# Decoder layer on one Trainium2 core: three folded FFN tiles instead of four

## The chip, the cores and the metric

One core of a Trainium2 chip runs the whole layer in one launch. The metric is device time in microseconds of that core. The runs shown are three of the kernel before, median 1054.19 (1053.89 to 1054.98). One execution was recorded by the hardware profiler; it took 1052.81.

The engines are called as in the profile: PE is TensorE (PEld its weight loads), DVE is VectorE, ACT is ScalarE, POOL is GpSimd, SP is SyncE, which only issues the weight transfers here.

## The reference, cut to what matters

A decoder layer for 272 tokens (16 meta tokens and 256) of width 2048: sparse attention and a pooling mixer, then an output projection with a residual and a layer norm, then a gated FFN with a causal convolution of width 3, and a second residual and layer norm. The part around the change:

```python
h = layer_norm(ALPHA * h + mix, ln1_g, ln1_b)
z = h @ w_up                                       # 2048 -> 2 * 5632
z = sum(zp[:, j:j + T] * conv_w[j] for j in range(3)) + conv_b
a, g = jnp.split(z, 2, axis=-1)
f = (jax.nn.gelu(a) * g) @ w_down
h = layer_norm(ALPHA * h + f, ln2_g, ln2_b)
```

## The kernel before, in words

Activations stand transposed, features on the 128 partitions and tokens along the row; 258 of the tokens are kept for the FFN. A matmul in full precision is made of three: weights and activations are split in a high and a low part, and high by high, high by low and low by high are summed in PSUM (lines 187 to 189 in `product`). A weight tile is 128 x 2048. SP loads it, and `fetch` splits it in two halves of 1024 columns: ACT copies the high part (line 123), DVE subtracts for the low part (line 124). The tiles come in one fixed stream, and `weights()` asks for each two places ahead of its use, from three buffers.

The FFN has 44 tiles of 128 hidden features. A tile `f` has two up-products of 48 matmuls, one for the value (`half_` 0) and one for the gate (`half_` 1). Then come the convolution (`conv`, lines 698 to 700: one ACT and two DVE instructions), the gelu and the product (`gate`, lines 715 and 716). Tiles are grouped in parts of eight. From the second part on the up-products alternate with down-products of the part before (lines 763 to 765). These take seven products where eight stand in the definition, from sums and differences of gated tiles. `forms` makes the sums for two tiles at a time: four instructions on POOL (735 to 738), then `two_parts`, the split of what they give, on ACT (721) and DVE (722). Their buffers are in two groups: `gp`, sixteen of them, and `acc`, one.

The layer norm before the FFN needs sums over all features, and they are known only when the output projection is done. So that PE need not wait, the first tiles are *folded*: their products take the unnormalised residual sum, multiplied by the norm's gain, of which sixteen split copies `folded` stand in the sixteen `gp` buffers (260 columns: two more for gain and bias). `unfold` then puts the token's scale and mean into the product: on DVE a copy of two columns (706) and a multiplication (708), on ACT an affine row (710, in the `acc` buffer), on POOL an addition (711). Meanwhile `normalise` makes the sixteen normalised parts `h_parts`, three after each product (lines 680 on POOL, 681 on DVE, 682 and 684 on ACT, 685 on DVE), and the tiles from `FOLDED` on read those.

After the tiles `FOLDED` and `FOLDED + 1` DVE transposes the residual in blocks, eight instructions each (line 860), and in the six tiles from `FOLDED + 2` on, 32 DMAs issued from ACT's queue (line 692) move the blocks to `y2`, where the down-products are summed. The first sums of part 0 are added to `y2` at the end of tile 9, and its other half is first read at the end of tile 11.

The program is written in this order, and each engine takes its instructions in a fixed order that a scheduler made of it; an instruction that waits holds up what stands behind it on its engine. These lines set where the change acts:

```python
if todo and f > FOLDED - 1 + half_:
    p, r = todo.pop(0)
    pairs[p].append(forms(r, len(pairs[p]), p == FAST))
if f < FOLDED:
    ...
    product(ps[:, :NE], hl, P, folded, 0, NE, k0=k)
    while len(h_parts) < min(KT, 3 * (2 * f + half_ + 1)):
        normalise(len(h_parts))
    ...
else:
    product(ps[:, :NQ], hl, P, h_parts, 0, NQ)
```

Of the kernel before, what the change touches and what calls it, by code (L numbers as in the profile page):

```python
# [33 lines left out]
FT = FF // P  # L34
PARTS = (8, 8, 8, 8, 8, 4)
FAST = 4
FOLDED = 4
MF = 80 + C
NE = NQ + 2
ALPHA = 2.0 ** 0.25  # L40
# [27 lines left out]
def tile_layer(ctx, tc, xt, w_first, w_proj, w_uk, w_uv, w_pool, w_o, w_up, w_down, cols, rows, rel_bias, onehot, out):  # L68
# [8 lines left out]
    def big():  # L77
        return pm.tile([P, 512], F32, tag="mm", name="mm")
# [652 lines left out]
    def forms(r, j, whole):  # L731

        a11, a21, a12, a22 = r[:, 0, :P], r[:, 0, P:], r[:, 1, :P], r[:, 1, P:]
        s = fp.tile([P, 4 * P], F32, name="forms", tag="acc", bufs=1).rearrange("p (a b) -> p a b", b=P)
        nc.gpsimd.tensor_tensor(s[:, 0], a21, a22, op=ALU.add)  # L735
        nc.gpsimd.tensor_tensor(s[:, 2], s[:, 0], a11, op=ALU.subtract)
        nc.gpsimd.tensor_tensor(s[:, 1], a12, s[:, 2], op=ALU.subtract)
        nc.gpsimd.tensor_tensor(s[:, 3], a11, a21, op=ALU.subtract)  # L738
        left = two_parts(slot(), r[:, :, :P])
        mid = two_parts(slot(), s[:, :2])  # L740
        right = ring.tile([P, 2, T], F32R, tag="act", name="right")
        right = two_parts(right[:, :, :2 * P].rearrange("p a (b c) -> p a b c", c=P), s[:, 2:])
        if j % 2 == 0:
            held["lone"], held["other"] = slot(), slot() if whole else None
        two_parts(held["lone"][:, :, j % 2], a22)
        if whole:
            two_parts(held["other"][:, :, j % 2], a21)
        return {"P1": (left, 0), "P2": (left, 1), "P5": (mid, 0), "P3": (mid, 1), "P6": (right, 0),
                "P7": (right, 1), "P4": (held["lone"], j % 2),
                "a11": (left, 0), "a12": (left, 1), "a21": (held["other"], j % 2), "a22": (held["lone"], j % 2)}  # L750
# [44 lines left out]
    for item in plan:  # L795
# [32 lines left out]
        ps = big()  # L828
# [4 lines that stand above are left out]
            k = 0  # L833
# [22 lines left out]
        elif f % 2:  # L856
            todo.append((part, pair))
        if f in (FOLDED, FOLDED + 1):
            for m in range(8 * (f - FOLDED), 8 * (f - FOLDED) + 8):
                nc.vector.transpose(y[:, m, NM:], y[:, m, NM:])  # L860
        if FOLDED + 2 <= f < FOLDED + 8:
            for _ in range((6, 5, 5)[f % 3]):
# [153 lines left out]
```

## Time and profile before

| what | value |
|---|---|
| median of three runs | 1054.19 us |
| the profiled execution, its time | 1052.81 us |
| the profiled execution, its span | 1051.0 us |
| granted TensorE clock over the span | 0.996 |
| first folded matmul | 306.7 us |
| first matmul that reads `h_parts` | 357.5 us |
| last matmul of the up-products | 993.6 us |
| moved by DMA, mean rate | 249.75 MB, 238 GB/s |

The span is the time from the first instruction to the last; the rest of the profiled execution's time lies around it. Rows of a timeline give start and duration in microseconds, engine, line, operation, the tile written and the tiles read, and in brackets the idle time of the engine before the instruction and what ended it. Matmuls are pipelined, and a duration of 0.28 is not the pace: that is read from start to start. Instructions of DVE overlap by some 0.08 in the same way. Groups of instructions give the busy time, the mean duration of one in ns and, behind the second bar, the idle time before them.

### The profile page before, as it was taken

The numbers are of one execution on the slowest core, as the hardware profiler recorded it, in microseconds if no ns is written. First come the engines' busy times: TensorE is split into PE (matmuls) and PEld (weight loads), VectorE is DVE, ScalarE is ACT, GpSimd is POOL, SyncE is SP. The second block draws the span as 40 slices with busy tenths as digits, with TensorE's granted clock in tenths as the row PEclk, the third lists the DMA queues.
The fourth block names the chain that finished last, engine by engine and source line by source line (L and its number), as shares of the span: only waits on it lengthen the run. The fifth ranks groups of instructions, "written<-read, shape, count | busy, mean of one in ns | idle before, by whom it ended". The sixth has DMA issues, their size and how long they took to land. (4 is left out here: it accounts for less than half of the span.)

```text
span 1051.0 us, 19241 instructions
## 1 busy us (share of the span) xinstructions
PE 1037.5 (99%) x7671; PEld 986.4 (94%) x7671; DVE 888.7 (85%) x1381; ACT 620.7 (59%) x998; POOL 214.0 (20%) x264
## 2 busy tenths in 40 slices
PE   9999999999999999999999999999999999999996
PEld 8998999999999999999999999999999999999985
DVE  6879468858779987898999989898998998989876
ACT  7666345745447765565665655556655665556673
POOL 1100014125436231201112021120211221220030
PEclk9999999999999999999999999999999999999998
DMA  9756542454552577898897787877878778788764
GB/s 322 255 172 237 190 152 96 148 189 164 193 193 89 201 217 213 276 310 261 275 300 270 284 275 264 289 274 270 284 268 290 270 281 275 271 280 272 285 210 141
DMA packets 59322, 249.75 MB, mean 238 GB/s; under 512 B 21686, under 2 KB 22112, under 8 KB 32224
## 3 DMA queue, kind: packets, MB, share of 16 engines
q1 hardware_dynamic: 34160, 229.76, 60.5%
q0 software_dynamic: 7600, 15.62, 7.8%
q10 hardware_dynamic: 17472, 3.15, 1.6%
q8 instruction: 60, 0.98, 0.4%
q14 instruction: 30, 0.25, 0.1%
HBM read 232.50 MB, written 2.11 MB: 223 GB/s over the span
## 5 line engine op out<-in xcount | busy, mean ns | idle before, releaser
L124 DVE TENSOR_TENSOR whl<-wraw,whl 128x1024 fp32r<-128x1024 f32 (+1 forms) x416 | 489.2, 1212 | 49.0 <-ACT whl L123 46.8
L123 ACT ACTIVATE whl<-wraw 128x1024 fp32r<-128x1024 f32 (+1 forms) x416 | 402.6, 1015 | 120.3 <-DVE wraw L119 26.4
L188 PE MATMUL mm<-hp,whl 128*128 128x258 f32 x1280 | 362.4, 283 | 0.0
L189 PE MATMUL mm<-hp,whl 128*128 128x258 f32 x1280 | 361.3, 282 | 0.8 <-DVE whl L124 0.8
L187 PE MATMUL mm<-hp,whl 128*128 128x258 f32 x1280 | 361.5, 282 | 0.2 <-ACT whl L123 0.2
L187 PEld LDWEIGHTS mm<-hp,whl 128*128 128x128 f32 x1280 | 242.5, 189 | 3.6 <-ACT whl L123 0.4
L188 PEld LDWEIGHTS mm<-hp,whl 128*128 128x128 f32 x1280 | 242.7, 190 | 3.1
L189 PEld LDWEIGHTS mm<-hp,whl 128*128 128x128 f32 x1280 | 242.9, 190 | 1.0 <-DVE whl L124 1.0
L187 PE MATMUL mm<-xp,whl 128*128 128x256 f32 (+5 forms) x384 | 111.2, 290 | 0.0
L188 PE MATMUL mm<-xp,whl 128*128 128x256 f32 (+5 forms) x384 | 108.9, 284 | 0.0
L189 PE MATMUL mm<-xp,whl 128*128 128x256 f32 (+5 forms) x384 | 108.7, 283 | 0.0
L698 ACT ACTIVATE z<-mm,cv 128x256 f32<-128x256 f32 x40 | 22.6, 564 | 91.4 <-PE mm L189 90.5
L188 PEld LDWEIGHTS mm<-xp,whl 128*128 128x128 f32 x384 | 72.3, 188 | 0.8 <-issue 0.5
L187 PEld LDWEIGHTS mm<-xp,whl 128*128 128x128 f32 x384 | 72.4, 188 | 0.6
L189 PEld LDWEIGHTS mm<-xp,whl 128*128 128x128 f32 x384 | 72.4, 189 | 0.3 <-DVE whl L124 0.2
L738 POOL TENSOR_TENSOR forms<-za 128x128 f32<-128x128 f32 x20 | 26.4, 1321 | 221.8 <-DVE za L716 214.3
L764 PE MATMUL at<-whl,gp 128*128 128x512 f32 x180 | 71.2, 396 | 0.0
L765 PE MATMUL at<-whl,gp 128*128 128x512 f32 x180 | 71.1, 395 | 0.0
L763 PE MATMUL at<-whl,gp 128*128 128x512 f32 x180 | 71.0, 395 | 0.0
L698 ACT ACTIVATE za<-mm,cv 128x256 f32<-128x256 f32 x40 | 22.5, 562 | 58.4 <-PE mm L189 58.4
L735 POOL TENSOR_TENSOR forms<-za 128x128 f32<-128x128 f32 x20 | 21.8, 1089 | 104.4 <-DVE za L716 104.3
L765 PEld LDWEIGHTS at<-whl,gp 128*128 128x128 f32 x180 | 33.8, 188 | 8.0
(327 smaller groups left out, 1942.7 us busy)
## 6 DMA issues: line engine op xcount, KB each, us to landing
wraw<-in_w_up SPq DMA_DIRECT2D x88, 1024.0 KB, 5.1
wraw<-in_w_down SPq DMA_DIRECT2D x80, 1024.0 KB, 6.5
wraw<-in_w_proj SPq DMA_DIRECT2D x24, 1024.0 KB, 5.0
wraw<-in_w_o SPq DMA_DIRECT2D x16, 1024.0 KB, 4.8
y<-v POOLq DMA_DIRECT2D x27, 256.0 KB, 8.4
y<-u POOLq DMA_DIRECT2D x18, 256.0 KB, 4.8
wraw<-in_w_first SPq DMA_DIRECT2D x8, 304.0 KB, 5.3
x<-in_xt SPq DMA_DIRECT2D x1, 2176.0 KB, 8.7
```

What stands on the lines that cost most here:

```text
L123: nc.scalar.activation(hl[:, 0, c], raw[:, c], AF.Copy)
L124: nc.vector.tensor_tensor(hl[:, 1, c], raw[:, c], hl[:, 0, c].bitcast(F32), op=ALU.subtract)
L187: nc.tensor.matmul(ps, wh, ah, start=n == 0, stop=False)
L188: nc.tensor.matmul(ps, wh, al, start=False, stop=False)
L189: nc.tensor.matmul(ps, wl, ah, start=False, stop=n == KT - 1)
L698: nc.scalar.activation(z, src[:, 2:NQ], AF.Identity, bias=col(C_B, j), scale=col(C_W, 3 * j + 2))
L735: nc.gpsimd.tensor_tensor(s[:, 0], a21, a22, op=ALU.add)
L738: nc.gpsimd.tensor_tensor(s[:, 3], a11, a21, op=ALU.subtract)
L763: nc.tensor.matmul(ps, a[:, 0, i], hl[:, 0, w], start=j == 0, stop=False)
L764: nc.tensor.matmul(ps, a[:, 0, i], hl[:, 1, w], start=False, stop=False)
L765: nc.tensor.matmul(ps, a[:, 1, i], hl[:, 0, w], start=False, stop=j == n - 1)
```

## The change

One constant:

```diff
-FOLDED = 4
+FOLDED = 3
```

By it, the products of tile 3 (the fourth) read `h_parts`, 258 columns, and not `folded`, 260; its two `unfold` calls go, and `conv` reads the PSUM directly, as in the later tiles. The `forms` of tiles 0 and 1 are called before the first product of tile 3 and not of tile 4, those of tiles 2 and 3 before the first of tile 4 and not of tile 5; from the pair of tiles 4 and 5 on the calls stand as before. The sixteen transpositions of the residual come after tiles 3 and 4 (before: 4 and 5), and the 32 moves in the tiles 5 to 10 (before: 6 to 11). The `normalise` calls stay where they were: three after each of the first five products and the sixteenth after the second product of tile 2. The order of the weight stream and of PE's products is the same.

## The prediction

> **Names.** Tiles are counted from 0, as `f` is in the code: the change takes tile 3 out of the folded ones. A tile has two products, 3a and 3b for tile 3. A product is 48 matmuls: for each of 16 operands three, the third of which reads the low part of the weights.
>
> **What bounds the kernel now.** I read the page's totals first, then the table by stretches.
>
> ```profile
> PE 1037.5 (99%) x7671; PEld 986.4 (94%) x7671; DVE 888.7 (85%) x1381; ACT 620.7 (59%) x998; POOL 214.0 (20%) x264
> ```
>
> ```profile
> 300.00:350.00 50.00, 49.37 (x407) 48.44 (x405) 43.68 (x84) 33.40 (x61) 23.77 (x25) 1.00 0.40 132
> 350.00:400.00 50.00, 48.88 (x403) 48.25 (x402) 45.03 (x79) 32.40 (x53) 14.46 (x17) 1.00 0.70 221
> 400.00:450.00 50.00, 50.00 (x365) 47.46 (x364) 42.71 (x59) 29.36 (x43) 9.29 (x10) 1.00 0.83 253
> ```
>
> The columns of the stretches are microseconds, then busy time of PE, PEld, DVE, ACT, POOL, then clock, DMA share and GB/s. TensorE works 99% of the span at a granted clock of 1.00, and from 400 us on it has no gap. The changed code lies between 300 and 400, the only stretch hereabouts where it misses time (0.63 and 1.12 us). Whatever start tile 6 gets is therefore carried to the end. So I forecast one number, the start of 6a. The timeline of PE shows where each product begins:
>
> ```profile
> 345.68 0.28 PE L187 MATMUL mm<-fold,whl 128*128 128x260 f32 x1
> ...
> 351.08 0.28 PE L187 MATMUL mm<-fold,whl 128*128 128x260 f32 x1
> ...
> 351.43 0.29 PE L187 MATMUL mm<-fold,whl 128*128 128x260 f32 x1
> ...
> 351.90 0.39 PE L189 MATMUL mm<-fold,whl 128*128 128x260 f32 x1
> ...
> 357.54 0.28 PE L187 MATMUL mm<-hp,whl 128*128 128x258 f32 x1
> ...
> 369.01 0.29 PE L187 MATMUL mm<-hp,whl 128*128 128x258 f32 x1
> ...
> 375.23 0.39 PE L187 MATMUL mm<-hp,whl 128*128 128x258 f32 x1 [0.24 <-ACT whl L123]
> ...
> 376.55 0.39 PE L189 MATMUL mm<-hp,whl 128*128 128x258 f32 x1 [0.82 <-DVE whl L124]
> ...
> 382.15 0.28 PE L187 MATMUL mm<-hp,whl 128*128 128x258 f32 x1
> ```
>
> These are the starts of 3a (345.68) with its sixteenth operand (351.08), of 3b, 4a, 5a, 5b and 6a. 4a and 4b together take 369.01 - 357.54 = 11.47, so a product that waits for nothing takes 5.74. Against that, 3b took 6.11 (its third matmul waited for weights) and 5b began 0.48 late and took 6.92. The waits to be won are thus 0.37 + 0.48 + 1.18 = 2.03 us, all for weights that ACT (L123) and VectorE (L124) split too late. VectorE is the engine behind them:
>
> ```profile
> 348.10 0.42 DVE L685 TENSOR_TENSOR hp<-x,hp 128x258 fp32r<-128x258 f32 x1
> ...
> 350.66 2.32 DVE L124 TENSOR_TENSOR whl<-wraw,whl 128x1024 fp32r<-128x1024 f32 x2
> 352.89 0.97 DVE L685 TENSOR_TENSOR hp<-x,hp 128x258 fp32r<-128x258 f32 x1
> ...
> 364.53 1.41 DVE L860 STREAM_TRANSPOSE x<-x 128x256 f32<-128x256 f32 x4
> ...
> 371.83 0.42 DVE L722 TENSOR_TENSOR gp<-forms,gp 128x256 fp32r<-128x256 f32 x1 [1.76 <-ACT gp L721]
> ...
> 373.71 0.43 DVE L860 STREAM_TRANSPOSE x<-x 128x256 f32<-128x256 f32 x1
> ...
> 374.38 0.47 DVE L699 SCALAR_TENSOR_TENSOR za<-mm,cv,za 128x256 f32<-128x256 f32 x1
> ...
> 375.28 2.35 DVE L124 TENSOR_TENSOR whl<-wraw,whl 128x1024 fp32r<-128x1024 f32 x2
> 377.55 0.42 DVE L722 TENSOR_TENSOR gp<-forms,gp 128x256 fp32r<-128x256 f32 x1
> ```
>
> Its only long idle time is 1.76 us before 371.83, where it stands behind the forms of tiles 0 and 1; the weights of 5b are split after that, at 375.28, and 5b is the product that waits.
>
> **What goes.** Tile 3's two unfoldings take these away, twice each:
>
> ```profile
> L711 POOL TENSOR_TENSOR u<-u,w 128x258 f32<-128x258 f32 x8 | 10.4, 1306 | 29.1 <-ACT w L710 18.4 <-DVE u L708 9.4 <-issue 1.3
> L710 ACT ACTIVATE w<-of_token,sc 128x258 f32<-128x258 f32 x8 | 4.8, 598 | 0.8 <-DVE sc L706 0.7
> L708 DVE TENSOR_TENSOR u<-mm,of_token 128x258 f32<-128x258 f32 x8 | 3.3, 412 | 0.0
> ```
>
> That is 2 x 1.31 us of POOL, 2 x 0.60 of ACT and 2 x 0.41 of VectorE (the two-column copy of L706 beside it is smaller). The 96 matmuls of tile 3 are 258 columns wide instead of 260; 3a from 345.68 to 351.43 took 5.75 with 260, a free product 5.74 with 258, so this is worth at most 0.02. None of the removed work stands on PE's path by itself; it counts through the order of the weight splits, below.
>
> **What is added: 3a now reads the normalised parts.** Up to the sixteenth part the order of the instructions on ACT, VectorE and POOL is the same in both kernels, and nothing in front of it waits for 3a. So its times can be read off:
>
> ```profile
> 351.81 0.41 ACT L684 ACTIVATE hp<-x 128x258 fp32r<-128x258 f32 x1
> ...
> 353.62 0.60 ACT L698 ACTIVATE za<-u,cv 128x256 f32<-128x256 f32 x1 [0.45 <-POOL u L711]
> ```
>
> High part at 351.81 + 0.41 = 352.22, low part at 352.89 + 0.97 = 353.86. 3a wants the operand at 351.08 and its low part one matmul, 0.12, later. The fifteenth part and those ahead of it come before the pair of L124 at 350.66, in time. So 3a stands until 353.9, and 3b begins at about 354.15 instead of 351.43: **+2.72**.
>
> Then the wait of 3b goes, for its weights are split by 350.66 + 2.32 = 352.98: 4a begins at 354.15 + 5.74 = 359.89, **+2.35**. If nothing else waited, 5b would begin at 359.89 + 3 x 5.74 = 377.11 and 6a at 382.85, **+0.70**.
>
> **What is moved.** The forms of tiles 0 and 1 now stand at 3a, those of tiles 2 and 3 at 4a; the sixteen transposes stand behind tiles 3 and 4. What is queued behind each is a weight split, so I follow VectorE to the split of 5b. First the rows of POOL, then two of ACT:
>
> ```profile
> 352.03 1.55 POOL L711 TENSOR_TENSOR u<-u,w 128x258 f32<-128x258 f32 x1 [6.39 <-ACT w L710]
> 354.85 1.16 POOL L711 TENSOR_TENSOR u<-u,w 128x258 f32<-128x258 f32 x1 [1.27 <-ACT w L710]
> ...
> 368.46 1.33 POOL L735 TENSOR_TENSOR forms<-za 128x128 f32<-128x128 f32 x1
> ...
> 370.88 0.46 POOL L737 TENSOR_TENSOR forms<-za,forms 128x128 f32<-128x128 f32 x1
> ```
>
> ```profile
> 354.13 0.59 ACT L710 ACTIVATE w<-of_token,sc 128x258 f32<-128x258 f32 x1
> 354.62 1.05 ACT L123 ACTIVATE whl<-wraw 128x1024 fp32r<-128x1024 f32 x1
> ```
>
> 1. ACT ends L698 at 354.22, as before, but in the new order one half of 4a's weights (1.05) stands between it and L710 (0.59): L710 ends near 355.7. POOL's add of tile 2b, 1.16 to 1.55, ends at 356.9 to 357.3. The four forms behind it take 370.88 + 0.46 - 368.46 = 2.88, and VectorE begins on them 371.83 - 371.34 = 0.49 after: at 360.3 to 360.7. It waits some 2 us there, as it did before 371.83.
> 2. From there to the end of tile 3's gate (L716) stand, in the new order: five small instructions that are the same five as from 371.83 to 373.71 (1.88); L699 and L700 with one transpose (0.90 from 374.38 to 375.28, and 0.35 from 1.41 / 4); the split of 4b (375.28 to 377.55, 2.27); seven transposes (2.45); L699, L700 and a transpose again (1.25); half the split of 5a (1.14); L716 (0.42). Sum 10.66; with 0.4 less where an instruction of the old rows stood behind POOL, 10.3. L716 ends at 370.6 to 371.4. On the way the first half of 4b's split is done by 360.7 + 1.88 + 1.25 + 1.22 = 365.05 at the latest, and 4b wants it with its third matmul, 365.63 + 0.24; that of 5a is done by 371.0, wanted at 371.6. Both are just in time.
> 3. Behind that gate stand the second forms. The same order of instructions is to be seen two tiles later:
>
> ```profile
> 387.17 0.42 DVE L716 TENSOR_TENSOR za<-za,z 128x256 f32<-128x256 f32 x1
> ...
> 392.58 2.36 DVE L124 TENSOR_TENSOR whl<-wraw,whl 128x1024 fp32r<-128x1024 f32 x2
> ```
>
> From L716's end at 387.59 to the end of the first half split, 392.58 + 1.22 = 393.80, it is 6.21, with a wait of VectorE for POOL and ACT inside. Here two transposes (0.70) stand in it as well: 6.9. So 5b's first half is there at 377.5 to 378.3. 5b wants it with its third matmul, 377.11 + 0.24 = 377.35: a wait of 0.15 to 0.95, with some 0.1 more to get going again. I take 0.8, towards the later end, as two forms and two transposes are more than the row behind the pattern had. 6a begins at 382.85 + 0.8: **+1.5 us**.
>
> The row of 352.89 shows a second thing: the L685 took 0.97 there and 0.42 at 348.10, and POOL's add ran from 352.03 to 353.58. [...]
>
> **Later.** Residual moves are issued one tile earlier from ACT's queue, as many as before. In the old trace the last of them hold VectorE up (the first row below) without reaching PE:
>
> ```profile
> 475.95 0.69 DVE L771 SCALAR_TENSOR_TENSOR y<-y,v 128x512 f32<-128x512 f32 x1 [1.91 <-issue]
> ...
> 477.75 2.36 DVE L124 TENSOR_TENSOR whl<-wraw,whl 128x1024 fp32r<-128x1024 f32 x2
> ...
> 479.39 0.28 PE L187 MATMUL mm<-hp,whl 128*128 128x258 f32 x1
> ```
>
> The split's first half was there at 478.9, wanted at 479.63: 0.7 us of cover, and I price the move at nothing. Were that cover gone, each microsecond that VectorE loses more would be lost to PE. The moves land a tile earlier, so the wait of 1.91 should go and the cover grow.
>
> **The sum.** The profiled execution took 1052.81, its span 1051.0 and 1.8 around it: 1054.3 with 1.5 more. The median of the runs is 1.38 above that execution, so I predict 1054.19 + 1.5 = **1055.7**.
>
> **Rivals.**
> - *No wait at 5b* (+0.7, 1054.9): the forms run as free on POOL as at 373, and 5b's split is there by 377.3. For it: the early end of my interval, 377.5, lies 0.15 behind that. Against: the only idle time of VectorE that could give way is the one behind the forms, and it gets a second one of that kind.
> - *Clearly slower*: not 3a's wait but the stand of ACT and VectorE behind POOL's forms, now in front of both 4b and 5b, sets the end. It passes 0.2% when 5b's first half ends after 378.65, 0.35 beyond my interval. [...]
> - *The parts come in time*: if 3a didn't wait and 5b's split came early too, 6a would begin at 357.54 + 4 x 5.74 = 380.50, that is -1.65: 1052.5. It needs both, and the row of 352.89 stands against it.
> - *Nothing changes* is excluded: the order of instructions does change from 353 on.
>
> **How the numbers follow.** A measurement of this kernel tells about 0.2% (2.1 us) from no change. Forecast (+1.0 to +2.1) 0.58; clearly slower 0.22; no wait at 5b 0.14; parts in time 0.06. The range leaves out the last, and the ends of both neighbours: 1054.2 to 1057.3. Slower by over 0.2% 0.22; faster by over 0.2% 0.03, as even the best case gives 1.65; within, 0.75.
>
> **What would show it.** Right: a gap of about 2.7 us in PE at the last operand of 3a, 4b and 5a without a gap, a gap under 1 us at 5b, no other up to 1000. Wrong: no gap at 3a (then the parts weren't late), a gap over 1.5 us in 4b to 5b (then the forms decide), or any gap after 400 (then the moved order of VectorE or the residual's moves count).

## The result and the profile after

| kernel | median us | lowest to highest | runs |
|---|---|---|---|
| before | 1054.04 | 1052.62 to 1054.98 | 6 |
| after | 1061.36 | 1060.74 to 1063.84 | 6 |

The ratio is 1.0079 with a 95% interval of 1.0069 to 1.0089: some 7.3 us slower, where 1.5 was predicted. The profiled execution of the kernel after took 1063.84, the longest of the six, and its span is 1062.1; that of before took 1.2 less than its median. So the two traces differ by 11.1 us, more than the medians.

First the totals of the page of after, then its table by stretches; the columns are those explained in the prediction. The last row is from the kernel before.

```profile
PE 1040.5 (98%) x7671; PEld 988.6 (93%) x7671; DVE 887.6 (84%) x1377; ACT 620.3 (58%) x996; POOL 208.9 (20%) x262
```

```profile
350.00:400.00 50.00, 47.67 (x382) 47.26 (x382) 44.02 (x76) 31.29 (x51) 13.05 (x15) 0.97 0.67 215
400.00:450.00 50.00, 49.10 (x359) 46.16 (x358) 33.45 (x45) 26.92 (x40) 7.42 (x10) 1.00 0.77 223
450.00:500.00 50.00, 45.36 (x308) 42.45 (x309) 43.30 (x63) 25.06 (x35) 5.75 (x7) 0.97 0.81 261
500.00:1000.00 500.00, 500.00 (x3569) 471.68 (x3569) 456.89 (x630) 298.23 (x415) 86.68 (x93) 1.00 0.81 277
```

```profile
450.00:500.00 50.00, 50.00 (x359) 47.21 (x359) 43.56 (x58) 28.68 (x40) 6.27 (x8) 1.00 0.90 282
```

Between 400 and 500, where TensorE had no gap before, it now misses 0.90 and 4.64 us, and the clock is 0.97 from 350 to 400 and from 450 to 500. From 500 to 1000 nothing is lost. VectorE does less in 400 to 450 (33.45, before 42.71): it stood still there.

**At 3a** the timeline of PE in after shows what the prediction said:

```profile
351.24 0.28 PE L189 MATMUL mm<-hp,whl 128*128 128x258 f32 x1
352.59 0.38 PE L187 MATMUL mm<-hp,whl 128*128 128x258 f32 x1 [1.07 <-ACT hp L684]
354.24 0.39 PE L188 MATMUL mm<-hp,whl 128*128 128x258 f32 x1 [1.26 <-DVE hp L685]
354.46 0.28 PE L189 MATMUL mm<-hp,whl 128*128 128x258 f32 x1
354.58 0.28 PE L187 MATMUL mm<-hp,whl 128*128 128x258 f32 x1
...
361.89 0.28 PE L187 MATMUL mm<-hp,whl 128*128 128x258 f32 x1
...
384.92 0.28 PE L187 MATMUL mm<-hp,whl 128*128 128x258 f32 x1
```

PE waits for the high and then for the low part of the sixteenth operand: from 351.24 to 354.24 it is 3.00 us for two steps that take 0.12 each otherwise: 2.76 lost, and the step after them takes 0.10 more. But 3b, from 354.58 to 361.89, takes 7.31 and not 5.74, though it waits for nothing. The same table in finer stretches, still of after:

```profile
355.00:356.00 1.00, 1.00 (x8) 1.00 (x8) 1.00 (x4) 1.00 (x3) 0.00 (x0) 0.74 0.89 352
356.00:358.00 2.00, 2.00 (x12) 2.00 (x11) 1.96 (x2) 1.37 (x2) 1.82 (x2) 0.50 0.68 287
358.00:359.00 1.00, 1.00 (x7) 1.00 (x7) 1.00 (x2) 0.46 (x2) 1.00 (x2) 0.56 0.00 0
```

PE counts as busy throughout, but the granted clock is 0.50 from 356 to 358: for (0.26 + 1.00 + 0.44) / 0.5 = 3.4 us TensorE ran at half clock, and 3b lost 7.31 - 5.74 = 1.57. From 361.89 to 384.92 it is 23.03 for four products: nothing waits at 4b, 5a or 5b. 6a starts 2.77 after that of before, 0.31 of it from ahead of 3a (its start is 345.99, before 345.68).

**After 400** PE stops three times, each time at a matmul of a down-product that reads the low part of its weights (L764):

```profile
431.54 0.39 PE L764 MATMUL at<-whl,gp 128*128 128x512 f32 x1
432.42 0.50 PE L764 MATMUL at<-whl,gp 128*128 128x512 f32 x1 [0.49 <-DVE whl L124]
...
449.19 0.39 PE L763 MATMUL at<-whl,gp 128*128 128x512 f32 x1
452.93 0.49 PE L764 MATMUL at<-whl,right 128*128 128x512 f32 x1 [3.35 <-DVE whl L124]
...
470.05 0.40 PE L763 MATMUL at<-whl,gp 128*128 128x512 f32 x1
472.15 0.50 PE L764 MATMUL at<-whl,right 128*128 128x512 f32 x1 [1.71 <-DVE whl L124]
```

The pace at 512 columns is 0.23 (four steps from 453.26 to 454.20 in after), so 0.65 + 3.51 + 1.87 = 6.03 us are lost, all to the low parts of weights, which VectorE makes. VectorE's own rows, from the timeline of after, tell why they were late:

```profile
424.15 0.43 DVE L716 TENSOR_TENSOR za<-za,z 128x256 f32<-128x256 f32 x1
429.40 0.69 DVE L115 TENSOR_TENSOR wraw<-wraw 128x512 f32<-128x512 f32 x1 [4.82 <-DMA wraw<-in_w_down]
430.01 4.63 DVE L124 TENSOR_TENSOR whl<-wraw,whl 128x1024 fp32r<-128x1024 f32 x4
...
449.60 0.69 DVE L118 TENSOR_TENSOR wraw<-wraw 128x512 f32<-128x512 f32 x1 [3.47 <-DMA wraw<-in_w_down]
...
451.66 4.09 DVE L124 TENSOR_TENSOR whl<-wraw,whl 128x1024 fp32r<-128x1024 f32 x4
...
469.54 0.69 DVE L118 TENSOR_TENSOR wraw<-wraw 128x512 f32<-128x512 f32 x1 [4.04 <-DMA wraw<-in_w_down]
```

Before a down tile is split, `fetch` forms differences of its raw columns (L115 for one kind, L118 to L120 for the other). I call that the pre-subtraction. It needs the tile's transfer. In the queue of after it stands, three times, **ahead of the splits of the two tiles before**, and VectorE waits 4.82, 3.47 and 4.04 us for a transfer while four split instructions stand behind it. ACT had the high parts of all four ready:

```profile
425.00 3.90 ACT L123 ACTIVATE whl<-wraw 128x1024 fp32r<-128x1024 f32 x4 [1.92 <-DVE za L716]
```

In the kernel before the splits come first at this place:

```profile
422.48 0.42 DVE L716 TENSOR_TENSOR za<-za,z 128x256 f32<-128x256 f32 x1
422.81 3.76 DVE L124 TENSOR_TENSOR whl<-wraw,whl 128x1024 fp32r<-128x1024 f32 x3
427.43 0.69 DVE L115 TENSOR_TENSOR wraw<-wraw 128x512 f32<-128x512 f32 x1 [0.86 <-DMA wraw<-in_w_down]
```

Its pre-subtraction waits for the same transfer, until 427.43. With the 2.77 that after is behind, that would be 430.20, and after had the tile at 429.40. So this transfer is not late; what stands behind the wait differs. VectorE stood idle for 4.82 us in front of work that could have been done.

At the second stop the transfer is late too, as a consequence of the first. SP issues it when a split has freed a buffer: here the split ends at 439.65 + 2.36 = 442.01 and the issue is at 442.04. These are the split and the issue in after, then the issue in the kernel before:

```profile
439.65 2.36 DVE L124 TENSOR_TENSOR whl<-wraw,whl 128x1024 fp32r<-128x1024 f32 x2 [1.96 <-ACT whl L123]
```

```profile
442.04 0.33 SPq L110 DMA_DIRECT2D wraw<-in_w_down  x1
```

```profile
434.94 0.33 SPq L110 DMA_DIRECT2D wraw<-in_w_down  x1
```

The issue comes 7.10 later, and only 2.77 + 0.65 = 3.42 of that is PE's lag so far; the rest is the work that VectorE had put off at the first stop.

The second stop is followed by another 3.4 us of half clock (the table of after shows 0.52 from 455 to 458), in which 16 matmuls of 258 columns take 0.22 each and not 0.12: some 1.5 more. The sum: 0.31 + 2.86 + 1.57, less the 2.03 of old waits that are gone, is 2.7 of the 2.77 up to 6a; 6.03 + 1.5 come after 400; and one wait at 1031 is 0.6 longer. With the 2.77 that is 10.9 of the 11.1.

### The profile page after: what moved, and what is told of

It is laid out like the page before. It is cut to its first block, busy times and chain, and to the rows that moved or that the text cites. A ratio compares the mean times of both kernels' runs of the same rounds, so it can differ in the third digit from the quotient of the medians.

```text
span 1062.1 us, 19233 instructions
## 1 busy us (share of the span) xinstructions
PE 1040.5 (98%) x7671; PEld 988.6 (93%) x7671; DVE 887.6 (84%) x1377; ACT 620.3 (58%) x996; POOL 208.9 (20%) x262
## 5 line engine op out<-in xcount | busy, mean ns | idle before, releaser
L188 PE MATMUL mm<-hp,whl 128*128 128x258 f32 x1312 | 373.0, 284 | 1.3 <-DVE hp L685 1.3
L187 PE MATMUL mm<-hp,whl 128*128 128x258 f32 x1312 | 372.0, 284 | 1.1 <-ACT hp L684 1.1
L189 PE MATMUL mm<-hp,whl 128*128 128x258 f32 x1312 | 371.8, 283 | 0.0
L188 PEld LDWEIGHTS mm<-hp,whl 128*128 128x128 f32 x1312 | 250.3, 191 | 4.5 <-DVE hp L685 1.5
L187 PEld LDWEIGHTS mm<-hp,whl 128*128 128x128 f32 x1312 | 250.0, 191 | 4.4 <-ACT hp L684 1.3
L189 PEld LDWEIGHTS mm<-hp,whl 128*128 128x128 f32 x1312 | 250.5, 191 | 0.1
L764 PE MATMUL at<-whl,gp 128*128 128x512 f32 x180 | 71.3, 396 | 0.5 <-DVE whl L124 0.5
```

What stands on the lines that cost most here:

```text
L187: nc.tensor.matmul(ps, wh, ah, start=n == 0, stop=False)
L188: nc.tensor.matmul(ps, wh, al, start=False, stop=False)
L189: nc.tensor.matmul(ps, wl, ah, start=False, stop=n == KT - 1)
L764: nc.tensor.matmul(ps, a[:, 0, i], hl[:, 1, w], start=False, stop=False)
```

## The experiments

Two causes were open. **Theory 1 (order)**: the scheduler's order on VectorE makes the stops after 400. **Theory 2 (queue)**: the residual's moves, which start a tile earlier, hold ACT or the transfers, whatever the order is. Times are medians beside the kernel before on the same chip, which was 1053.6 to 1054.0 each time; ratios carry 95% intervals.

| run | us | ratio to before | PE stops from 400 to 500 |
|---|---|---|---|
| after | 1061.36 | 1.0079 (1.0069 to 1.0089) | three |
| e1_pin | 1055.55 | 1.0014 (1.0006 to 1.0023) | none |
| e2_products | 1054.81 | 1.0010 (1.0001 to 1.0019) | none |
| e3_turn | 1062.47 | 1.0073 (1.0059 to 1.0087) | three |
| e4_half | 1053.79 | 1.0001 (0.9993 to 1.0010) | none |
| e5_order_alone | 1062.70 | 1.0094 (1.0081 to 1.0108) | three |
| e6_moves_late | 1056.14 | 1.0020 (1.0012 to 1.0029) | none |
| e7_half_early_pin | 1052.88 | 0.9994 (0.9985 to 1.0003) | none |
| e9_turn_held | 1053.28 | 0.9996 (0.9987 to 1.0004) | none |
| e10_held_alone | 1053.76 | 1.0000 (0.9992 to 1.0009) | none |
| e11_half_spread | 1053.29 | 0.9990 (0.9980 to 1.0000) | none |

### e1_pin: the changed kernel with the pre-subtractions held back

```diff
+        if kind:
+            with tc.issue_after(state["split"]):
+                if kind == "A":
+                    nc.vector.tensor_tensor(b12, b12, b11, op=ALU.subtract)
...
+        state["split"] = nc.cur_bb.bb.instructions[-1]
```

`issue_after` tells the scheduler to place what stands in it behind the instruction named, here the last split of the tile before. The three lines of the other kind are held in the same way.

> The changed kernel with one thing more: the subtractions that prepare a raw weight tile for the folded down products on VectorE are held until the split of the tile before has been issued, so that none stands ahead of older tiles' splits. The scheduler may place ScalarE's copies anew as well. Theory 1 (order): the stops of TensorE at 431, 449 and 470 us and the second clock drop at 454 come from a pre-subtraction that waits for its weight tile with the splits of two older tiles behind it. Then TensorE has no gap over 0.3 us between 400 and 1000, the clock record at 454 is gone, and what is left is the wait at 3a with its clock drop at 355: 1056.5 (1055.8 to 1057.2). Theory 2 (queue): the residual's moves, one tile earlier, hold ScalarE or the transfers whatever VectorE's order is: the gaps stay and the time is 1060 to 1062.

1055.55 us, 5.8 below the median of the changed kernel, which was not run beside it. The table by stretches of this kernel:

```profile
400.00:450.00 50.00, 50.00 (x366) 47.50 (x365) 39.07 (x54) 27.09 (x40) 7.21 (x9) 1.00 0.74 226
450.00:500.00 50.00, 50.00 (x360) 47.21 (x359) 45.69 (x64) 30.27 (x40) 7.04 (x8) 1.00 0.91 302
```

PE has no gap and the clock is 1.00, with the moves as early as in after. Theory 2 expected 1060 to 1062. The time is 0.25 under theory 1's own range of 1055.8 to 1057.2; its profiled execution has the half clock after 3a, and the next run shows that not all executions have it. ACT's copies were placed anew too, so this run alone would not tell VectorE's order from ACT's.

### e2_products and e8_products_again: three folded tiles, everything else late

```diff
+TURN, MOVE, FORMS = 4, 6, 4
...
-        if todo and f > FOLDED - 1 + half_:
+        if todo and f > FORMS - 1 + half_:
...
-        if f in (FOLDED, FOLDED + 1):
-            for m in range(8 * (f - FOLDED), 8 * (f - FOLDED) + 8):
+        if f in (TURN, TURN + 1):
+            for m in range(8 * (f - TURN), 8 * (f - TURN) + 8):
...
-        if FOLDED + 2 <= f < FOLDED + 8:
+        if MOVE <= f < MOVE + 6:
```

> Three folded tiles as in the changed kernel, but the residual's turning, its moves and the half sums start where the kernel before has them. Theory 1: 3a waits 2.8 us and the clock halves at 355 as in the changed kernel, no gap over 0.3 us after 400: 1056.5 (1055.8 to 1057.2). Theory 2 gives the same, since the moves are late again. If the product edit itself (less slack after 385) made the later gaps, they stay: 1060 to 1062.

> The same kernel as the second run of this study, once more, for the clock: if the half clock after 3a's stop of 2.8 us is a matter of chance between executions, its record at about 355 us may be there this time, and then 3b takes 7.2 us instead of 5.7; if it depends on the kernel, the clock is 1.00 there again. The stop itself is 1.33 + 1.64 us either way.

e2 took 1054.81; e8 is one more execution of the same program, on another chip (1055.53). No gap stands between 400 and 1000 in either, so the product edit doesn't make the later stops. e2 was faster than expected; in its profiled execution (1054.50) the clock had not fallen. PE at 3a, then stretches of the table, first of e2, then of e8:

```profile
352.42 0.38 PE L188 MATMUL mm<-hp,whl 128*128 128x258 f32 x1 [1.05 <-ACT hp L685]
354.06 0.39 PE L189 MATMUL mm<-hp,whl 128*128 128x258 f32 x1 [1.26 <-DVE hp L686]
```

```profile
355.00:356.00 1.00, 1.00 (x11) 1.00 (x10) 1.00 (x3) 1.00 (x3) 0.06 (x1) 1.00 0.98 410
```

```profile
351.96 0.39 PE L188 MATMUL mm<-hp,whl 128*128 128x258 f32 x1 [1.06 <-ACT hp L685]
353.61 0.58 PE L189 MATMUL mm<-hp,whl 128*128 128x258 f32 x1 [1.25 <-DVE hp L686]
```

```profile
351.00:355.00 4.00, 1.78 (x7) 1.58 (x8) 4.00 (x8) 2.92 (x7) 1.53 (x1) 0.78 0.46 141
355.00:356.00 1.00, 1.00 (x7) 1.00 (x6) 1.00 (x2) 1.00 (x2) 0.53 (x1) 0.50 0.97 410
```

The stop is the same to 0.01 us, and the clock is 1.00 in one execution and 0.50 in the other. The eleven executions of e2, all on one chip, part as well: four have a granted clock of 0.997 over the span and take 1053.31 to 1054.50, seven have 0.994 to 0.996 and take 1054.71 to 1057.37. So the half clock after 3a is a matter of the execution and not of the kernel; the last section has what the traces show of it. In the profiled e2 6a begins at 383.24, and 3a 0.13 later than in the kernel before: without the clock, the product edit costs 383.24 - 382.15 - 0.13 = 0.96 us.

### e3_turn: only the residual's turning and its moves early, four folded tiles

```diff
+TURN, MOVE, FORMS = 3, 5, 4
...
-        if f in (FOLDED, FOLDED + 1):
-            for m in range(8 * (f - FOLDED), 8 * (f - FOLDED) + 8):
+        if f in (TURN, TURN + 1):
+            for m in range(8 * (f - TURN), 8 * (f - TURN) + 8):
...
-        if FOLDED + 2 <= f < FOLDED + 8:
+        if MOVE <= f < MOVE + 6:
```

> Four folded tiles as before; only the residual's transposes and moves begin one tile earlier (fourth tile). Both theories: 6a starts near 382.2 as before, and the three gaps between 430 and 475 are there, since the scheduler's order on VectorE has the three early pre-subtractions here too and the moves are early too: 1060 to 1062. If the gaps need the product edit, 1054 to 1054.5.

1062.47 us, so the loss after 400 comes without the product edit. (The profiled execution took 1058.22, the least of the six, so its trace shows less than the median; where the others lose 4 us more is not shown.) One row of its table:

```profile
400.00:450.00 50.00, 47.17 (x337) 43.87 (x336) 36.00 (x50) 28.06 (x41) 7.34 (x9) 1.00 0.75 222
```

PE misses 2.83 us there, with stops at 428 and 446 that lose 0.42 and 2.73. The third, at 466, loses only 0.24 in this execution.

### e6_moves_late: the changed kernel with only the moves late

```diff
+TURN, MOVE, FORMS = 3, 6, 3
...
-        if FOLDED + 2 <= f < FOLDED + 8:
+        if MOVE <= f < MOVE + 6:
```

> The changed kernel (three folded tiles, transposes and half sums early), with only the residual's moves a tile later, where the kernel before has them. VectorE's order has none of the three early pre-subtractions. If the moves' place is what makes the scheduler choose the other order: no gap over 0.3 us between 400 and 1000, 1054.8 (1054.3 to 1056.3, the upper end with a half clock at 355). If the transposes' place makes it: gaps as in the changed kernel, 1060 to 1062.

1056.14 us and no gap after 400. Between this kernel and the changed one stands only the tile in which the 32 moves begin. So, with the transposes early, it is the moves' place that makes the scheduler choose the other order; the transposes and the half sums by themselves don't. The moves early by themselves were not run. The median is 1.3 over that of e2 on another chip, with intervals that overlap (1.0012 to 1.0029, 1.0001 to 1.0019); the profiled execution has its clock at 1.00 after 3a.

### e5_order_alone: the kernel before with only the order forced

```diff
+LATE = (65, 69, 73)
...
+        if i in LATE:
+            first = nc.cur_bb.bb.instructions[-1]
+            for r, h, cs in held_splits:
+                with tc.issue_after(first):
+                    for c in cs:
+                        nc.vector.tensor_tensor(h[:, 1, c], r[:, c], h[:, 0, c].bitcast(F32), op=ALU.subtract)
+            held_splits.clear()
...
-            nc.vector.tensor_tensor(hl[:, 1, c], raw[:, c], hl[:, 0, c].bitcast(F32), op=ALU.subtract)
+            if i is None or not {i + 1, i + 2} & set(LATE):
+                nc.vector.tensor_tensor(hl[:, 1, c], raw[:, c], hl[:, 0, c].bitcast(F32), op=ALU.subtract)
+        if i is not None and {i + 1, i + 2} & set(LATE):
+            held_splits.append((raw, hl, cs))
```

> The kernel before with four folded tiles and its late turning and moves; only VectorE's order is forced into the changed kernel's: at three weight tiles of the down products (66th, 70th and 74th of the stream, about 430, 450 and 470 us) the subtraction that prepares the raw tile stands ahead of the splits of the two tiles before it. The scheduler may place ScalarE's copies anew. Theory 1 (order): stops of TensorE of 0.4 to 4 us at about 430, 450 and 470 us, each behind a pre-subtraction that waits for its transfer: 1058 to 1062. Theory 2 (the residual's early moves hold ScalarE or the transfers): no stop over 0.3 us there, 1054.

1062.70 us, 0.7 over the range of theory 1, with nothing of the change in it. VectorE's timeline of this kernel at the first of the three tiles:

```profile
426.33 0.69 DVE L117 TENSOR_TENSOR wraw<-wraw 128x512 f32<-128x512 f32 x1 [4.21 <-DMA wraw<-in_w_down]
426.94 4.63 DVE L128 TENSOR_TENSOR whl<-wraw,whl 128x1024 fp32r<-128x1024 f32 x4
```

It is the pair of rows of after: wait for the transfer, then four splits at a run. PE stops at 428, 447 and 467 us. ACT is no rival for the first stop: around it its rows come, by line, in the same order in this kernel, before and after (a convolution row, four copies, a convolution row, two copies). For the two later stops ACT's order differs and was not held apart.

### e9_turn_held and e10_held_alone: the early moves, and the hold by itself

e9 is e3 with the hold of e1, e10 the kernel before with that hold and nothing else.

> The third run's kernel (four folded tiles, transposes and moves one tile early) with the pre-subtractions held behind the split of the tile before. If the early moves cost only through VectorE's order: no gap over 0.3 us between 400 and 1000, 1053.5 to 1054.5 beside 1062.5 without the hold. If the early moves take something from the transfers or from ScalarE as well: 1055 to 1058.

> The control: the kernel before with nothing but the hold on the pre-subtractions. If the hold only forbids the bad order, which the kernel before does not have, it is worth nothing: 1053.5 to 1054.5. If the hold by itself makes VectorE's queue better, 1052 to 1053.4, and then the last runs with the hold read too low by as much.

e9 took 1053.28 where e3 took 1062.47 (on two chips, on which the kernel before took 1053.95 and 1053.63); e10 is even with the kernel before, so the hold is worth nothing of its own. The table of e9:

```profile
400.00:450.00 50.00, 50.00 (x366) 47.48 (x365) 40.57 (x58) 28.03 (x43) 7.24 (x9) 1.00 0.80 241
450.00:500.00 50.00, 50.00 (x360) 47.19 (x359) 44.35 (x60) 30.40 (x41) 7.04 (x8) 1.00 0.91 299
```

The early moves are free as long as the order is kept. Theory 2 falls. What the runs leave open is the scheduler's reason: which instruction's changed place made it move three pre-subtractions forward was not traced.

### e4_half, e7_half_early_pin and e11_half_spread: candidates

Here the first product of tile 3 stays folded and its second takes the normalised parts; all three have this edit:

```diff
-        if f < FOLDED:
+        if f < FOLDED and (f, half_) != (FOLDED - 1, 1):
...
+            if f < FOLDED:
+                both = [conv(f, 0, unfold(both[0]), pair[:, f % 2])]
```

e7 has the half sums, transposes and moves early as in the changed kernel and the hold of e1; e11 is e7 with the second eight transposes after tile 5 and the moves from tile 6 on.

> A split between both kernels: the first product of the fourth tile takes the unnormalised sum and is unfolded, its second product takes the normalised parts; the residual's turning, its moves and the half sums as before. If the cost at 385 is the wait of 3a alone, with its clock drop: the last part is there for 3b, no gap over 0.5 us between 340 and 385, no half clock at 355, and the waits of the kernel before at 3b, 5a and 5b (0.37, 0.48, 1.18) are partly gone: 1052.0 to 1054.0. If the parts are no earlier for 3b than it can use them, 3b waits some 0.5 to 2 us: 1054 to 1056.

> A candidate: the first product of the fourth tile folded, its second on the normalised parts (no wait of 2.8 us at 3a), everything that the change moves early, and the pre-subtractions held behind the split of the tile before. If 3a's wait is all that the early product costs and VectorE keeps up as it did in the first run of this study (no wait at 4a to 5b), 6a starts near 380.5 to 381.5 instead of 382.15: 1052.0 to 1053.5. If VectorE is the bound in this stretch, the waits come back at 4b to 5b and it is 1053.5 to 1055, as with the half kernel before it.

> A candidate: as the seventh run (half a folded fourth tile, forms early, hold), but the second eight transposes stand behind the sixth tile instead of the fifth, and the moves start one tile later for it. In the seventh run VectorE did three transposes between the forms and the split that 5b waited for (1.38 us). If these make the wait, it shrinks by about 1.1 us: 1051.8 to 1052.8. If VectorE's stand behind POOL's forms makes it, it stays: 1052.5 to 1053.5.

e4 is even with the kernel before. 3a's wait and the half clock are gone, but 5a and 5b wait 0.99 and 1.38 us. e7 and e11 read 1.0 and 0.7 us below the kernel before on their chips; the interval of e7 holds 1, that of e11 ends on it, so neither is shown to be faster. In both 5b still waits; the row is from e7's PE:

```profile
376.14 0.38 PE L192 MATMUL mm<-hp,whl 128*128 128x258 f32 x1 [1.22 <-DVE whl L126]
```

And this is VectorE ahead of that split in e11:

```profile
372.40 0.42 DVE L725 TENSOR_TENSOR gp<-forms,gp 128x256 fp32r<-128x256 f32 x1 [1.35 <-ACT gp L724]
...
373.28 0.76 DVE L865 STREAM_TRANSPOSE x<-x 128x256 f32<-128x256 f32 x2
...
374.33 0.43 DVE L865 STREAM_TRANSPOSE x<-x 128x256 f32<-128x256 f32 x1
...
375.05 2.35 DVE L126 TENSOR_TENSOR whl<-wraw,whl 128x1024 fp32r<-128x1024 f32 x2
```

Three transposes still stand there in e11, though the second eight were moved; so it did not tell its two cases apart.

## Why the prediction was wrong, point by point

- **3a's wait, +2.72: right.** 2.73 to 2.76 was lost there in the five profiled executions that have it, to the operand's high part and then its low part, as worked out from the unchanged order up to it.
- **4b and 5a without a wait: right.** They follow at the free pace, to within 0.1 for all four products.
- **The wait of 0.8 at 5b: wrong, there was none.** I had 5b's first half ready at 377.5 to 378.3 and wanted at 377.35. In e6, which has the changed kernel's order up to there and no half clock, VectorE splits it here:

```profile
376.53 2.35 DVE L125 TENSOR_TENSOR whl<-wraw,whl 128x1024 fp32r<-128x1024 f32 x2
```

  With 1.22 for the first half it is there at 377.75, less the 0.39 by which e6 runs behind the kernel before (3a starts at 346.07): 377.36, 0.14 ahead of the early end of my interval and just in time; PE reads it at 378.01 in e6 without a wait. The working took the later end on the ground that two transposes stand in it; the early end was the better one. So the rival "no wait at 5b" (+0.7) was the course of the product edit: +0.96 in the profiled e2 and, by the same working, +0.97 in e6 (6a at 383.51). The median of e2, whose executions by their granted clock mostly have the half clock, is 1.2 over the kernel before (ratio 1.0010, or 0.1 to 2.0 us).
- **"A product that waits for nothing takes 5.74": not so after a stop.** 3b took 7.31, since the granted clock fell to 0.50 for 3.4 us after 3a's stop. I priced the stop and not the clock behind it: 1.57 in the profiled execution of after.
- **"I price the move at nothing": the step that failed.** It looked at the moves' arrival, which was not the trouble, and not at what their place does to the scheduled order. Between 400 and 500 VectorE's queue had been reordered at three tiles: 6.03 us of stops and some 1.5 of clock in the profiled execution, and 9.2 us between the medians of e3 and e9. The ground that I gave was weak too: the row of the 1.91 ends with "<-issue", so it doesn't show that a move held VectorE up. (In after the same instruction, at 478.01, has no wait.) The prediction followed the new order as far as the split of 5b and stopped there.
- **"Whatever start tile 6 gets is carried to the end": right only as a lower bound.** That PE had no gap after 400 in the old trace says that the order of before had cover, not how much cover the new one has. The last part of the prediction had named a gap after 400 as the sign that the moved order of VectorE or the residual's moves count; of these two it was the order, brought about by the moves' place.
- **"Clearly slower"** came about, but not as that rival had it: no wait at 4b or 5b was over 0.1 us.

## What to carry to other kernels

Where a scheduler fixes each engine's queue, compare each engine's whole queue before and after, not only up to the edit: look for an instruction that waits for a transfer and has been put ahead of work whose inputs are already there. Its price is its wait less the cover of what stands behind it, here 4.82 us of wait for 0.65 of loss at one tile and, with the cover used up, 3.47 for 3.51 at the next. Where such an order appears as a side effect, holding the waiting instruction behind the older work (e9, e10) takes the loss away and costs nothing.

## What the runs showed of the hardware

After a stop of TensorE of about 3 us the granted clock stood at 0.50 for 3.4 us, in some executions only. Of five executions with 3a's stop (2.97 to 3.00 us from start to start, with one matmul in the middle) three show it (after, e1, e8) and two don't (e2, e6). Stops of 2.63 and 2.87 us in e5, 2.96 in e3 and 3.74 in after were followed by it; the one of 2.10 at 470 in after was not. Its onset varies: in after it began 1.2 us after the stop's end (355.48 and 354.24), in e8 some 0.3 before it (353.28 and 353.61).

Neither the stop's length nor PE's idle time in it parts the executions of 3a's stop. PE stood idle for 1.07 + 1.26 = 2.33 us in after and 1.06 + 1.25 = 2.31 in e8, where the clock fell, and for 1.05 + 1.26 = 2.31 in e2, where it did not. What decides whether a stop of this length is followed by the half clock is not shown.
